# Which head of the attention keeps its norm temporaries apart: from the last one to the second last

## The chip, the cores and the metric

The kernel runs on one core of a Trainium2 chip. The core has five engines with queues of their own: TensorE (PE, matrix products, which it writes to PSUM), VectorE (DVE), ScalarE (ACT), GpSimd (POOL) and SyncE (SP, which here only starts transfers). They run side by side and wait for each other by semaphores. The metric is the device time of one launch in microseconds; a change is judged by the median of its runs beside those of the kernel before.

## The reference

One block of a streaming encoder on 512 rows of width 2048, all in float32: a combined input projection, eight heads of stick-breaking attention, eight heads of forgetting attention, a norm of each head's output, an output projection with residual, and a feed-forward part with squared relu.

```python
def head_rmsnorm(o, g):
    of = o.astype(jnp.float32)
    of = of * lax.rsqrt(jnp.mean(of * of, axis=-1, keepdims=True) + EPS)
    ...

h = rmsnorm(x, g_attn[l])
proj = jnp.einsum('bsd,de->bse', h, w_in[l])
...
o_sb = stick_breaking_attention(qa, ka, va)
o_fox = forgetting_attention(qf, kf, vf, log_f)
mixed = jnp.concatenate([head_rmsnorm(o_sb, g_out_sb[l]),
                         head_rmsnorm(o_fox, g_out_fox[l])], axis=-1)
x = x + jnp.einsum('bse,ed->bsd', mixed, w_out[l])

h2 = rmsnorm(x, g_mlp[l])
u = jax.nn.relu(jnp.einsum('bsd,df->bsf', h2, w_up[l]))
x = x + jnp.einsum('bsf,fd->bsd', u * u, w_down[l])
...
return rmsnorm(x, g_final)
```

## The kernel before

Each float32 operand is split into a high part and the rest: `split` (L56 to L64) lets ScalarE cast the high part (L59) and VectorE subtract it (L60). A product is then three matmuls, high by high, high by low and low by high (`mm3`, L82 to L85). In the profile a product's three matmuls thus carry the lines L83, L84 and L85 whatever they compute, and the tile written tells which: `accv` is the projection to v, `accq` that to q and k, `o` or `oq` the weighted sum of v, `acco` the output projection, `accu` the up and `accd` the down projection.

The heads go in pairs, in the order written in `order`: the eight forgetting heads first, then the stick-breaking heads 0 to 7, so heads 6 and 7 are the last pair. For each head `scores` makes the scores, ScalarE, VectorE and GpSimd turn them into weights `w` in an SBUF tile, and `weigh` (from L213) does the rest:

- TensorE transposes the weights into the PSUM tile `pt` (L218).
- `split` puts them into `ph` (ScalarE, L59) and `pl` (VectorE, L60), each 128 x 1280.
- Twelve matmuls multiply them with v into `o` (L231). For the last head the result is the first bank of a PSUM tile `oq`, whose second bank later takes the sum of squares.
- The head's norm: `os` is the copy of the result (ScalarE, L242), `sq` its square (VectorE, L243), split into `sh` and `sl`; two matmuls with a matrix of ones sum it over the head (L247, L248); `va` is the mean (VectorE, L249); `rsqrt` computes Ln and Exp on ScalarE (L89, L90) and a refining step on VectorE (L91 to L93) in `ra`, `sq` and `va`; the last operation writes `mixed[:, h]` (L251).

`mixed` is the operand of the output projection. That stage takes four blocks of 512 columns, and in each of them eight steps of two heads in the same `order`: weights are loaded and split (`wh`, `wl`), the two heads are split (`uh`, `ul`), and each of four accumulators (one for each 128 rows) takes two times three matmuls. At the end of a block VectorE adds the sums to the residual (L446), ScalarE squares them (L448), and TensorE transposes the new rows (L424) for the next stage.

Tiles come from pools. `wide(name)` gives a tile of 128 x 1280 with a tag of that name from the pool `at`, which holds one buffer for a tag: a new `ph` can be written only when the last reader and writer of the `ph` before is done. In `weigh`, all heads but the last take a second `ph` and `pl` (`n1` and `n2`) for the norm: the first halves hold `sq` and `sh`, the second halves `va` and `sl`. Their `os` and `ra` lie in the tags `ul4` and `uh5` of the pool `up`. The last head has six tiles of 128 x 512 of its own, `os_last` to `sl_last`.

No order is written out by hand: a scheduler puts each engine's instructions in a fixed order when the program is built, by priorities (attention is marked with a high one) and an estimate of its own of when things are ready. That order cannot change on the chip. So the output projection's first matmuls stand between those of the last heads' weighing and norms.

Of the kernel before, what the change touches and what calls it, by code (L numbers as in the profile page):

```python
# [8 lines left out]
F32 = mybir.dt.float32  # L9
F32R = mybir.dt.float32r  # L10
# [4 lines left out]
P = 128  # L15
NT = 512
# [3 lines left out]
NH = 8  # L20
# [16 lines left out]
def block_kernel(ctx, tc, x, g_attn, w_in, b_f, g_out_sb, g_out_fox, w_out, g_mlp, w_up, w_down, g_final, y):  # L37
# [19 lines left out]
    def split(hi, lo, src, scale=None):  # L57
        if scale is None:
            ins = act.copy(hi, src)  # L59
            lows[0] = dve.tensor_tensor(lo, src, hi.bitcast(F32), op=ALU.subtract)  # L60
        else:
            ins = act.mul(hi, src, scale)  # L62
            dve.scalar_tensor_tensor(lo, src, scale, hi.bitcast(F32), op0=ALU.mult, op1=ALU.subtract)
        return ins  # L64
# [5 lines left out]
    def load_w(src, a, b):  # L70

        raw = wp.tile([P, a, b], F32, tag="wraw", name="wraw")
        sp.dma_start(raw, src)
        out = []
        per = min(a, 2 * NT // b)
        for i in range(0, a, per):
            hi, lo = (w.rearrange("p (a b) -> p a b", a=per) for w in hi_lo(per * b))
            split(hi, lo, raw[:, i:i + per, :])
            out += [(hi[:, j, :], lo[:, j, :]) for j in range(per)]
        return out  # L80

    def mm3(out, sh, sl, mh, ml, first, last):  # L82
        pe.matmul(out, sh, mh, start=first, stop=False, skip_group_check=True)  # L83
        pe.matmul(out, sh, ml, start=False, stop=False, skip_group_check=True)  # L84
        pe.matmul(out, sl, mh, start=False, stop=last, skip_group_check=True)  # L85

    def rsqrt(out, v, a, b):

        act.activation(a, v, AF.Ln)  # L89
        act.activation(a, a, AF.Exp, scale=-0.5)  # L90
        dve.scalar_tensor_tensor(b, a, -0.5, v, op0=ALU.mult, op1=ALU.mult)  # L91
        dve.tensor_tensor(b, b, a, op=ALU.mult)
        dve.scalar_tensor_tensor(out, b, 1.5, a, op0=ALU.add, op1=ALU.mult)  # L93
# [29 lines left out]
    g_up, g_sb, g_fx = g_rest[:, :KC], g_rest[:, KC:KC + NH], g_rest[:, KC + NH:]  # L123
# [10 lines left out]
    with (  # L134
# [17 lines left out]
        def accumulate_v(c0, m, steps, prepare=None, more=None):  # L152

            per = NT // m
            banks = [acc.tile([P, NT], F32, tag="acc", name="accv") for _ in range(2)]
            if more is not None:
                banks += [more.tile([P, NT], F32, tag="more", name="accm") for _ in range(2)]
            ps = [banks[t // per][:, t % per * m:(t % per + 1) * m] for t in range(TB)]
            k1 = 0
            for step in steps:  # L160
                k0, k1 = k1, k1 + step
                if prepare is not None:
                    prepare(k0, step)
                w = load_w(w_in[k0 * P:(k0 + step) * P, c0:c0 + m].rearrange("(a p) c -> p a c", p=P), step, m)
                for t in range(TB):
                    ts = slice(t * P, (t + 1) * P)
                    for i in range(step):
                        k = k0 + i
                        mm3(ps[t], hH[:, k, ts], hL[:, k, ts], *w[i], k == 0 and t % per == 0, k == KC - 1)
            return ps  # L170

        def take_v(ps):
            vh = at.tile([P, TB, 2 * P], F32R, tag="vh", name="vh", bufs=2)
            vl = at.tile([P, TB, 2 * P], F32R, tag="vl", name="vl", bufs=2)
            for t in range(TB):
                split(vh[:, t, :], vl[:, t, :], ps[t][:, :2 * P], r1[:, t:t + 1])
            return vh, vl
# [15 lines left out]
        def wide(name, dt=F32):  # L193
            return at.tile([P, 1280], dt, tag=name, name=name)

        def scores(q, k):
            s = atp.tile([P, 1536], F32, tag="s", name="s")
            for i in (3, 2, 0, 1):
                n = (i + 1) * P
                qs = slice(i * P, (i + 1) * P)  # L200
                mm3(s[:, OFF_Q[i]:OFF_Q[i] + n], q[0][:, qs], q[1][:, qs], k[0][:, :n], k[1][:, :n], i != 0, True)
            return s[:, :1280]

        def rows(w):
            return [w[:, OFF_Q[i]:OFF_Q[i] + (i + 1) * P] for i in range(TB)]

        def causal(w, op, fill):

            for d, n in ((w[:, P:1280].rearrange("p (a b) -> p a b", b=384)[:, :, 256:], 3), (w[:, 896:1024], 1)):
                pool.affine_select(out=d, in_=d, compare_op=op, fill=fill, base=0,  # L210
                                   pattern=[[0, n], [-1, P]] if n > 1 else [[-1, P]], channel_multiplier=1)

        def weigh(h, v, hc, w, gv, last=False):  # L213

            pt = atp.tile([P, 1536], F32, tag="s", name="pt")
            for j in range(TB):
                for i in range(j, TB):
                    pe.transpose(pt[:, OFF_T[j] + (i - j) * P:OFF_T[j] + (i - j + 1) * P],  # L218
                                 w[:, OFF_Q[i] + j * P:OFF_Q[i] + (j + 1) * P], ident)
            ph, pl = wide("ph", F32R), wide("pl", F32R)  # L220
            split(ph, pl, pt[:, :1280])
            hs = slice(hc * P, (hc + 1) * P)
            if last:
                oq = atp.tile([P, 1536], F32, tag="s", name="oq")
                o, q = oq[:, :NT], oq[:, NT:2 * NT]
            else:
                o = atp.tile([P, NT], F32, tag="o", name="o")
            for j in range(TB):
                n = NT - j * P
                js = slice(OFF_T[j], OFF_T[j] + n)  # L230
                mm3(o[:, j * P:], v[0][:, j, hs], v[1][:, j, hs], ph[:, js], pl[:, js], j == 0, j == TB - 1)  # L231
            if last:
                os_, sq, va, ra = (at.tile([P, NT], F32, name=f"{c}_last") for c in ("os", "sq", "va", "ra"))
                sh, sl = (at.tile([P, NT], F32R, name=f"{c}_last") for c in ("sh", "sl"))
            else:
                os_ = up.tile([P, NT], F32, tag="ul4", name="os")
                ra = up.tile([P, NT], F32, tag="uh5", name="ra")
                n1, n2 = wide("ph"), wide("pl", F32R)
                sq, va = n1[:, :NT], n1[:, NT:2 * NT]
                sh, sl = n2[:, :NT], n2[:, NT:2 * NT]  # L240
                q = None
            act.copy(os_, o)  # L242
            dve.tensor_tensor(sq, os_, os_, op=ALU.mult)  # L243
            split(sh, sl, sq)
            if q is None:
                q = atp.tile([P, NT], F32, tag="o", name="ssq")
            pe.matmul(q, onesr, sh, start=True, stop=False)  # L247
            pe.matmul(q, onesr, sl, start=False, stop=True)  # L248
            dve.tensor_scalar(va, q, 1.0 / P, EPS, op0=ALU.mult, op1=ALU.add)  # L249
            rsqrt(va, va, ra, sq)  # L250
            dve.scalar_tensor_tensor(mixed[:, h, :], os_, gv, va, op0=ALU.mult, op1=ALU.mult)  # L251

        def attend_sb(h, v, hc, q, k):
            s = scores(q, k)
            w = wide("w")
            act.activation(w, s, AF.Abs)
            act.activation(w, w, AF.Exp, scale=-1.0)
            act.activation(w, w, AF.Ln, bias=1.0)
            dve.scalar_tensor_tensor(w, s, 0.0, w, op0=ALU.max, op1=ALU.add)
            causal(w, ALU.is_gt, 0.0)  # L260
            for r in rows(w):

                dve.tensor_tensor_scan(r[:, ::-1], r[:, ::-1], r[:, ::-1], 0.0, op0=ALU.add, op1=ALU.max)
            dve.tensor_tensor(w, s, w, op=ALU.subtract)
            act.activation(w, w, AF.Exp)
            causal(w, ALU.is_gt, 0.0)
            weigh(h, v, hc, w, g_sb[:, h:h + 1], h == order[-1])

        def attend_fox(h, v, hc, q, k):
            ck = atp.tile([P, NT], F32, tag="o", name="ck")  # L270
# [21 lines left out]
        order = [NH + h for h in (6, 7, 0, 1, 2, 3, 4, 5)] + list(range(NH))  # L292

        def v_columns(h):
            return 2 * WSB + h * P if h < NH else o0 + 2 * WSB + (h - NH) * P
# [61 lines left out]
        with tc.tile_pool(name="attp", bufs=1, space=PSUM) as atp:  # L357
# [9 lines left out]
            v = take_v(ps)  # L367
# [21 lines left out]
            for n in range(0, 2 * NH, 2):  # L389
# [11 lines left out]
                if n:  # L401
                    v = take_v(accumulate_v(v_columns(order[n]), 2 * P, [4] * 4))
# [25 lines left out]
    for n in range(4):  # L428
        ns = slice(n * NT, (n + 1) * NT)
        ps = [acc.tile([P, NT], F32, tag="acc", name="acco") for _ in range(TB)]  # L430
        for k0 in range(0, 2 * NH, 2):
            e0 = order[k0]
            w = load_w(w_out[e0 * P:(e0 + 2) * P, ns].rearrange("(a p) c -> p a c", p=P), 2, NT)
# [141 lines left out]
    for g in range(NG):  # L575
        for db in range(2):
# [6 lines left out]
            for j, p in enumerate(ORDER):  # L583
                if j in steps:
                    job.step()
                w = b_form(p, b)
# [129 lines left out]
```

## Time and profile before

| | |
|---|---|
| median of 3 runs | 2152.41 us (2151.77 to 2153.89) |
| the profiled execution | 2151.46 us |
| its span, first to last instruction | 2149.4 us |
| TensorE busy | 2131.2 us, 99% of the span |
| VectorE busy | 1402.8 us, 65% |
| ScalarE busy | 881.0 us, 41% |
| GpSimd busy | 63.2 us, 3% |
| TensorE's mean granted clock | 0.998 |

In the profile, `out<-in` names the tile written and those read; an instruction's row gives its start in us from the start of the span, its duration, engine, line and operation, and in brackets the idle time of that engine just before it with what ended it. The chain of waits goes back from the last instruction, at each step to what released it. Matmuls are pipelined: their durations overlap, and the distance from start to start tells how fast they follow each other.

### The profile page before, as it was taken

The numbers are of one execution on the slowest core, as the hardware profiler recorded it, in microseconds if no ns is written. First come the engines' busy times: TensorE is split into PE (matmuls) and PEld (weight loads), VectorE is DVE, ScalarE is ACT, GpSimd is POOL, SyncE is SP. The second block draws the span as 40 slices with busy tenths as digits, with TensorE's granted clock in tenths as the row PEclk, the third lists the DMA queues.
The fourth block names the chain that finished last, engine by engine and source line by source line (L and its number), as shares of the span: only waits on it lengthen the run. The fifth ranks groups of instructions, "written<-read, shape, count | busy, mean of one in ns | idle before, by whom it ended". The sixth has DMA issues, their size and how long they took to land.

```text
span 2149.4 us, 25658 instructions
## 1 busy us (share of the span) xinstructions
PE 2131.2 (99%) x10356; PEld 1801.0 (84%) x10356; DVE 1402.8 (65%) x1547; ACT 881.0 (41%) x1146; POOL 63.2 (3%) x75
## 2 busy tenths in 40 slices
PE   9999999999999999999999999999999999999997
PEld 8888988998997888888888888888888888888886
DVE  5455555766566554566776776766776776777788
ACT  6333333444345445443433333333433433433444
POOL 0000000000010000000000000000000000000005
PEclk9999999999999999999999999999999999999999
DMA  6333333322333324233333233233233233233323
GB/s 189 80 84 83 78 83 84 79 79 79 89 112 123 94 93 157 69 118 98 98 114 102 89 117 108 89 114 112 88 108 118 88 99 120 87 101 120 92 70 127
DMA packets 201366, 216.71 MB, mean 101 GB/s; under 512 B 6768, under 2 KB 156832, under 8 KB 201120
## 3 DMA queue, kind: packets, MB, share of 16 engines
q1 hardware_dynamic: 200288, 212.95, 32.9%
q10 hardware_dynamic: 960, 2.13, 0.3%
q8 instruction: 81, 1.33, 0.3%
q14 instruction: 37, 0.30, 0.0%
HBM read 210.86 MB, written 4.19 MB: 100 GB/s over the span
## 4 chain that ended last, share of the span: by engine, by line
PE 96%; DVE 2%; ACT 1%; DMA 1%; issue 0%; POOL 0%; SPq 0%; ACTq 0%; DVEq 0%
PE accu L83 11%; PE accu L84 11%; PE accu L85 11%; PE accd L85 9%; PE accd L83 9%; PE accd L84 9%; PE accq L85 5%; PE accq L83 5%; PE accq L84 5%; PE acco L83 3%; PE acco L84 3%; PE accv L83 3%; PE accv L85 3%; PE acco L85 3%; PE accv L84 3%; PE pt L218 1%
## 5 line engine op out<-in xcount | busy, mean ns | idle before, releaser
L59 ACT CAST wh<-wraw 128x1024 fp32r<-128x1024 f32 (+2 forms) x261 | 270.0, 1035 | 409.9 <-PE accd L85 153.7
L60 DVE TENSOR_TENSOR wl<-wraw,wh 128x1024 fp32r<-128x1024 f32 (+2 forms) x261 | 314.3, 1205 | 166.1 <-ACT wh L59 133.7
L564 DVE TENSOR_TENSOR m<-m,accd 128x1024 f32<-128x1024 f32 x204 | 248.7, 1219 | 263.4 <-PE accd L85 261.7
L83 PE MATMUL accu<-h2h,wh 128*128 128x512 f32 x1024 | 398.6, 389 | 0.0
L84 PE MATMUL accu<-h2l,wh 128*128 128x512 f32 x1024 | 398.4, 389 | 0.0
L85 PE MATMUL accu<-h2h,wl 128*128 128x512 f32 x1024 | 383.7, 389 | 0.0
L59 ACT CAST wh<-wd 128x1024 fp32r<-128x1024 f32 x210 | 219.6, 1052 | 273.6 <-PE accd L85 151.1
L83 PE MATMUL accd<-wh,ufh 128*128 128x512 f32 x840 | 326.8, 389 | 0.0
L84 PE MATMUL accd<-wl,ufh 128*128 128x512 f32 x840 | 326.8, 389 | 0.0
L85 PE MATMUL accd<-wh,ufl 128*128 128x512 f32 x840 | 326.8, 389 | 0.0
L60 DVE TENSOR_TENSOR wl<-wd,wh 128x1024 fp32r<-128x1024 f32 x210 | 255.1, 1221 | 15.1 <-ACT wh L59 13.8
L83 PEld LDWEIGHTS accu<-h2h,wh 128*128 128x128 f32 x1024 | 192.2, 188 | 39.9
L84 PEld LDWEIGHTS accu<-h2l,wh 128*128 128x128 f32 x1024 | 192.2, 188 | 39.8
L85 PEld LDWEIGHTS accu<-h2h,wl 128*128 128x128 f32 x1024 | 192.1, 188 | 39.9
L85 PE MATMUL accq<-hH,wl 128*128 128x512 f32 x512 | 200.8, 392 | 0.0
L83 PE MATMUL accq<-hH,wh 128*128 128x512 f32 x512 | 200.6, 392 | 0.0
L84 PE MATMUL accq<-hL,wh 128*128 128x512 f32 x512 | 200.4, 391 | 0.0
L84 PEld LDWEIGHTS accd<-wl,ufh 128*128 128x128 f32 x840 | 157.7, 188 | 32.8
L85 PEld LDWEIGHTS accd<-wh,ufl 128*128 128x128 f32 x840 | 157.6, 188 | 32.7
L83 PEld LDWEIGHTS accd<-wh,ufh 128*128 128x128 f32 x840 | 157.6, 188 | 32.7
L83 PE MATMUL accv<-wh,hH 128*128 128x256 f32 (+1 forms) x480 | 137.4, 288 | 0.7 <-ACT hH L62 0.7
L84 PE MATMUL accv<-wl,hH 128*128 128x256 f32 (+1 forms) x480 | 135.5, 284 | 0.0
(213 smaller groups left out, 2736.7 us busy)
## 6 DMA issues: line engine op xcount, KB each, us to landing
wraw<-in_w_up_dram SPq DMA_DIRECT2D x128, 512.0 KB, 3.7
wd<-in_w_down_dram SPq DMA_DIRECT2D x120, 512.0 KB, 3.6
wraw<-in_w_in_dram SPq DMA_DIRECT2D x92, 512.0 KB, 3.7
wraw<-in_w_out_dram SPq DMA_DIRECT2D x32, 512.0 KB, 3.6
m<-in_x_dram SPq DMA_DIRECT2D x4, 1024.0 KB, 11.9
wraw<-in_w_down_dram SPq DMA_DIRECT2D x8, 512.0 KB, 4.2
mixed<-in_x_dram SPq DMA_DIRECT2D x2, 1024.0 KB, 10.8
wraw<-in_w_in_dram SPq DMA_DIRECT2D x7, 264.0 KB, 6.8
```

Of the source, the lines that this page charges most:

```text
L59: ins = act.copy(hi, src)
L60: lows[0] = dve.tensor_tensor(lo, src, hi.bitcast(F32), op=ALU.subtract)
L83: pe.matmul(out, sh, mh, start=first, stop=False, skip_group_check=True)
L84: pe.matmul(out, sh, ml, start=False, stop=False, skip_group_check=True)
L85: pe.matmul(out, sl, mh, start=False, stop=last, skip_group_check=True)
L218: pe.transpose(pt[:, OFF_T[j] + (i - j) * P:OFF_T[j] + (i - j + 1) * P], w[:, OFF_Q[i] + j * P:OFF_Q[i] + (j + 1) * P], ident)
L564: dve.tensor_tensor(M[p][:, :, db, :], M[p][:, :, db, :], ps, op=ALU.add)
```

## The change

`weigh` is told how many heads are still to come (`left`) instead of whether its head is the last. For the last head (`left == 0`) only the output copy `os` and the factor `ra` get tiles of their own; its `sq`, `va`, `sh` and `sl` lie in a second `ph` and `pl` as those of the heads before. For the head before it (`left == 1`, head 6) `os` and `ra` stay in the pool `up`, and `n1` and `n2` get tiles of their own of 128 x 1024. All other heads are as before. What is computed does not change, and no instruction is added or removed. From the line of `act.copy(os_, o)` on, lines are one higher in the new file.

```diff
-        def weigh(h, v, hc, w, gv, last=False):
+        def weigh(h, v, hc, w, gv, left=2):
...
-            if last:
+            if left == 0:
                 oq = atp.tile([P, 1536], F32, tag="s", name="oq")
                 o, q = oq[:, :NT], oq[:, NT:2 * NT]
             else:
-                o = atp.tile([P, NT], F32, tag="o", name="o")
+                o, q = atp.tile([P, NT], F32, tag="o", name="o"), None
...
-            if last:
-                os_, sq, va, ra = (at.tile([P, NT], F32, name=f"{c}_last") for c in ("os", "sq", "va", "ra"))
-                sh, sl = (at.tile([P, NT], F32R, name=f"{c}_last") for c in ("sh", "sl"))
+            if left == 0:
+                os_, ra = (at.tile([P, NT], F32, name=f"{c}_last") for c in ("os", "ra"))
             else:
                 os_ = up.tile([P, NT], F32, tag="ul4", name="os")
                 ra = up.tile([P, NT], F32, tag="uh5", name="ra")
+            if left == 1:
+                n1, n2 = at.tile([P, 2 * NT], F32, name="n1"), at.tile([P, 2 * NT], F32R, name="n2")
+            else:
                 n1, n2 = wide("ph"), wide("pl", F32R)
-                sq, va = n1[:, :NT], n1[:, NT:2 * NT]
-                sh, sl = n2[:, :NT], n2[:, NT:2 * NT]
-                q = None
+            sq, va = n1[:, :NT], n1[:, NT:2 * NT]
+            sh, sl = n2[:, :NT], n2[:, NT:2 * NT]
...
-            weigh(h, v, hc, w, g_sb[:, h:h + 1], h == order[-1])
+            weigh(h, v, hc, w, g_sb[:, h:h + 1], NH - 1 - h)
```

## The prediction

> **What bounds the kernel now.** I read the page first, then what TensorE waits for over the whole run, then the chain of waits and the timeline around the one place found.
>
> ```profile
> span 2149.4 us, 25658 instructions
> PE 96%; DVE 2%; ACT 1%; DMA 1%; issue 0%; POOL 0%; SPq 0%; ACTq 0%; DVEq 0%
> ```
>
> The second line is the chain that ended last, by engine: 96% of the span is TensorE (PE) work. A change off TensorE's queue is worth only what TensorE stands still for it. All its recorded waits of the run are these five (total us, times, longest):
>
> ```profile
> PE trg L300 <- DMA g_rows<-in_g_attn_dram: 3.2, 1, 3.2
> PE acco L83 <- ACT uh L59: 2.1, 1, 2.1
> PE tr L149 <- DMA mixed<-in_x_dram: 1.0, 2, 0.8
> PE accv L83 <- ACT hH L62: 0.7, 2, 0.5
> PE acce L84 <- DVE wll L60: 0.4, 1, 0.4
> ```
>
> The first, third and fourth belong to the start, the fifth to the tail. The second is the only stall between them. The chain of waits across it (start, duration):
>
> ```profile
> 681.34 0.69 DVE sq_last L92
> ...
> 682.54 0.69 DVE va_last L93
> ...
> 684.28 0.76 DVE mixed L251
> 685.06 0.63 ACT uh L59
> 685.73 0.50 PE acco L83
> ```
>
> The names ending in `_last` are head 7's norm tiles, the last head in `order`. The output projection is already running (`acco`), and its last head needs `mixed[:, 7]`: L251 writes it, L59 casts it, and only then TensorE goes on. Timeline of TensorE there (start, duration):
>
> ```profile
> 678.06 0.39 PE L83 MATMUL acco<-wh,uh 128*128 128x512 f32 x1
> ...
> 683.27 0.39 PE L85 MATMUL acco<-wh,ul 128*128 128x512 f32 x1
> 685.73 0.50 PE L83 MATMUL acco<-wh,uh 128*128 128x512 f32 x1 [2.07 <-ACT uh L59]
> ...
> 687.68 1.07 PE L85 MATMUL acco<-wh,ul 128*128 128x512 f32 x4
> 688.85 0.66 PE L424 MATMUL tr<-ident,m 128*128 128x128 f32 x4
> ```
>
> Durations overlap, so I count starts. From 678.06 to 683.27 there are 23 steps: 5.21 / 23 = 0.2265 us a matmul. The matmul after 683.27 was due at 683.50 and started at 685.73: **2.23 us lost**. The twelve matmuls from 685.73 should take 2.72 us, but the transposes start 3.12 us later: **0.40 us more**. There the four accumulators end together (the last four matmuls are all L85), so the first transpose has to wait for VectorE's residual addition.
>
> Why head 7 is late:
>
> ```profile
> 660.15 0.75 DVE L251 SCALAR_TENSOR_TENSOR mixed<-os,g_rest,ph 128x512 f32<-128x512 f32 x1
> 660.93 1.23 ACT L59 CAST ph<-pt 128x1280 fp32r<-128x1280 f32 x1 [2.73 <-DVE mixed L251]
> 662.19 1.49 DVE L60 TENSOR_TENSOR pl<-pt,ph 128x1280 fp32r<-128x1280 f32 x1 [1.30 <-ACT ph L59]
> 668.43 0.39 PE L83 MATMUL oq<-ph,vh 128*128 128x512 f32 x1
> ...
> 670.29 0.44 PE L85 MATMUL acco<-wh,ul 128*128 128x512 f32 x1
> ```
>
> Head 6 keeps its norm temporaries (n1, n2) in the tiles `ph` and `pl`. Head 7's weights need the same two tiles, so the cast of head 7 waits until head 6 has written `mixed`. From there to TensorE's first `oq` matmul (668.43) and to the first matmul behind the group (670.29) head 7 is a whole norm behind.
>
> **The change part by part.**
>
> **Head 6's n1 and n2 in tiles of their own.** No instruction is added or removed; the twelve `oq` matmuls, the norm and its four sum matmuls stay. What goes is the wait of `ph<-pt` on L251. In the changed program's order that cast waits for TensorE alone, stands ahead of head 6's `os` copy on ScalarE, and the `oq` group stands 74 matmuls behind the last `accv` matmul instead of 149. So it is a move, and its cover has to be counted. Rows around the new place:
>
> ```profile
> 644.04 0.22 PE L85 MATMUL o<-ph,vl 128*128 128x128 f32 x1
> 644.30 0.59 ACT L242 COPY os<-o 128x512 f32<-128x512 f32 x1 [5.56 <-PE o L85]
> 644.81 1.32 ACT L59 CAST uh<-mixed 128x512 fp32r<-128x512 f32 x2
> 644.92 0.69 DVE L243 TENSOR_TENSOR ph<-os 128x512 f32<-128x512 f32 x1 [4.90 <-ACT os L242]
> 645.53 1.33 DVE L60 TENSOR_TENSOR ul<-mixed,uh 128x512 fp32r<-128x512 f32 x2
> 646.03 1.04 ACT L59 CAST wh<-wraw 128x1024 fp32r<-128x1024 f32 x1
> 647.11 1.23 DVE L60 TENSOR_TENSOR wl<-wraw,wh 128x1024 fp32r<-128x1024 f32 x1 [0.26 <-ACT wh L59]
> 650.75 0.39 PE L83 MATMUL acco<-wh,uh 128*128 128x512 f32 x1
> 651.43 0.39 PE L83 MATMUL acco<-wh,uh 128*128 128x512 f32 x1
> ...
> 654.63 0.63 ACT L89 ACTIVATE ra<-ph 128x512 f32<-128x512 f32 x1 [2.33 <-DVE ph L249]
> 655.29 0.63 ACT L90 ACTIVATE ra<-ra 128x512 f32<-128x512 f32 x1
> 655.94 1.30 ACT L59 CAST uh<-mixed 128x512 fp32r<-128x512 f32 x2
> ```
>
> The last reader of head 6's `ph` is the matmul at 644.04, so ScalarE begins head 7's cast at 644.30: 1.23 us, to 645.53. VectorE's `pl` (1.49 us) then ends near 647.1. The first 73 places hold matmuls of the same sizes in both programs, so place 74 is the start of 651.43: 4.3 us of slack. Queued behind the cast on ScalarE are `os` (0.59), two `uh` (1.32) and `wh` (1.04). The `uh` pair ends near 644.30 + 1.23 + 0.59 + 1.32 = 647.4; TensorE wants it at place 71, 650.75: 3.3 us of slack, the smallest. Behind `pl` on VectorE are head 6's square (0.69), two `ul` (1.33) and `wl` (1.23), done near 650.4; TensorE wants the `ul` only after the `oq` group, near 653.5 (651.43 plus that group's 1.86 us, 668.43 to 670.29). The delay of up to 2.8 us is thus hidden behind matmuls. Without that cover each us beyond 3.3 would stop TensorE. The bounds for this edit are a loss of 0 and one of 2.8 us if nothing covered it; I take 0, since the slack exceeds it.
>
> On ScalarE the copy `os_last<-oq` can now start only when `oq` has ended, near 653.6, and behind it stand head 6's Ln, Exp and the next `uh` pair. TensorE wants that pair at place 135, 48 steps behind the `oq` group: 653.5 + 48 × 0.2265 = 664.4. Copy, Ln, Exp and pair take 0.59 + 0.63 + 0.63 + 1.30 = 3.15 us by the rows above, with VectorE's square and average of head 6 or 7 in between (0.69 each), so they too are covered.
>
> The Trainium skill speaks against such a move: "TensorE: Matmul & The Clock Gate", in the paragraph on engine queue depths of Part 1, has ScalarE and VectorE as strict first-in first-out queues, and only TensorE pulling weight loads forward. By it a late `oq` would block every operand split behind it; if the engines could pass it, the loss would be 0 without any cover. The sum is made with the strict order, and the slack makes both come out alike; it is the slower rival that leans on the rule.
>
> **What the stall becomes.** From the end of `oq` to head 7's write of `mixed` took 684.28 − 670.29 = 14.0 us before. The same from 653.3 gives about 667. TensorE reaches head 7's part of the projection at 683.50, so the 2.23 us go, with some 15 us to spare. Nothing of head 7 is late next.
>
> **The last head's n1, n2 in `ph`, `pl`; its `os` and `ra` apart.** The same operations on other addresses: 0. Head 7's square needs `ph` free, that is its own `oq` matmuls done, which the copy before it already waits for. No later head wants the tiles. The new tiles take as much memory as the old (12 KB a partition), and the four loads of x keep their places in SP's queue; no queue is passed.
>
> **The edge between the first and second column block.** With head 7 in time, the projection's last step runs accumulator by accumulator, so the first addition is done eighteen matmuls before its transposes, and the 0.40 us go. The transposes then stand as four groups of four instead of 4, 4 and 8. The second edge of the old run has that pattern already:
>
> ```profile
> 694.73 0.48 PE L83 MATMUL acco<-wh,uh 128*128 128x512 f32 x1
> ...
> 734.29 0.60 PE L424 MATMUL tr<-ident,m 128*128 128x128 f32 x4
> ...
> 739.42 0.48 PE L83 MATMUL acco<-wh,uh 128*128 128x512 f32 x1
> ```
>
> It takes 5.13 us with 15 matmuls between; the first edge took 694.73 − 688.85 = 5.88 us with 18, which is 5.20 for 15: a gain of 0.07.
>
> **Sum.** 2.23 + 0.40 + 0.07 = 2.70 us. The profiled execution took 2151.46 us (2149.4 span and 2.06 around it), so it becomes 2148.76. It lies 0.95 below the median of the runs shown, 2152.41; on that scale the forecast is **2149.7 us**.
>
> **The rivals.** (a) *Hidden anyway:* the tail or a load takes the 2.7 us back, 2152.4. Against it stands that VectorE, the engine nearest to TensorE's load in the up/down stage, waits for TensorE:
>
> ```profile
> L564 DVE TENSOR_TENSOR m<-m,accd 128x1024 f32<-128x1024 f32 x204 | 248.7, 1219 | 263.4 <-PE accd L85 261.7
> ```
>
> 261.7 us of idle time ended by TensorE means that it starts earlier when TensorE does. For it: the tail is not TensorE's alone. 9%.
>
> (b) *Slower, the wait stays:* `ph` is not freed early after all, while TensorE's order already has `oq` at place 74. `pl` would end at 663.68 as now, TensorE would stand from 651.43 for 12.2 us, with the whole projection queued behind it: 2152.41 + 12.2 − 2.7 = 2161.9. It decides once the weights are more than 4.3 us later than worked out, and ends above the old time from 4.3 + 2.7 = 7.0. This is also the case that the change doesn't do what it says. The changed program's only wait at that cast is TensorE's, so 6%.
>
> (c) *More than the stall:* the gap also slowed what follows it, in the timed executions if not in the profiled one, which was the quickest of all (2151.46 against 2151.77 to 2153.89). The stretches of the profile, with TensorE's granted clock as the column before the last two:
>
> ```profile
> 683.50:685.73 2.23, 0.16 (x2) 0.00 (x1) 2.15 (x4) 1.21 (x2) 0.00 (x0) 1.00 0.20 13
> 685.73:689.30 3.57, 3.47 (x17) 2.62 (x17) 1.86 (x3) 1.14 (x2) 0.00 (x0) 1.00 0.39 139
> ```
>
> The clock stays at 1.00. Were some fifteen matmuls after the gap to run at half rate, that would be 15 × 0.2265 = 3.4 us more to gain: 2152.41 − 2.7 − 3.4 = 2146.3. 9%. "TensorE: Matmul & The Clock Gate" of the Trainium skill (Part 1) halves the clock after an idle window of about 3.4 us; the gap is shorter, and the row agrees.
>
> **How the numbers follow.** Forecast 76%, (a) 9%, (b) 6%, (c) 9%. A measurement of this kernel tells about 0.2%, 4.3 us, from no change. The forecast lies inside that; with runs that spread over 2.1 us, 10 of its 76 read beyond it. Faster: 10 + 9 = 19%. Same: 66 + 9 = 75%. Slower: 6%. The range takes in (a) and a spread of about 2 us below the forecast: 2147.6 to 2152.7, with (b) and most of (c) left out.
>
> **What would show it.** Right: no wait of `acco` on `uh` in the list of TensorE's waits; head 7's cast starting near 644.3 without VectorE as releaser; `oq` from about 651.4 to 653.3; head 7's L251 (a line later in the new file) near 667; the first transposes near 686.2 instead of 688.85, and every later stage earlier by 2.6 to 2.7. Wrong: a new wait of TensorE between 650 and 690, above all at `oq` or the first `uh` behind it, or an unchanged start of the tail.

## The result, and the profile after

| | median (us) | lowest to highest | runs |
|---|---|---|---|
| before | 2153.2 | 2151.77 to 2154.4 | 20 |
| changed | 2149.22 | 2148.45 to 2150.38 | 20 |

The ratio is 0.9982, 95% interval 0.9975 to 0.9989. The medians are 4.0 us apart and the means 3.8 us; the interval reaches from 2.4 to 5.4 us. The profiled execution took 2148.76 us against 2151.46, that is 2.70 less. So the profiled executions differ by the predicted sum, though not by its terms alone (the spans differ by 2.4 us, 2149.4 against 2147.0; more on this below), and the timed runs by about 1.1 us more. Most of what follows is about that remainder.

The page of the changed kernel, with the chain that ended last by engine, and its list of what TensorE waits for:

```profile
span 2147.0 us, 25661 instructions
PE 96%; DVE 2%; ACT 1%; issue 0%; POOL 0%; DMA 0%; SPq 0%; ACTq 0%; DVEq 0%
```

```profile
PE trg L301 <- DMA g_rows<-in_g_attn_dram: 3.3, 1, 3.3
PE tr L149 <- DMA mixed<-in_x_dram: 1.3, 2, 1.1
PE accv L83 <- ACT hH L62: 0.7, 2, 0.5
PE acce L84 <- DVE wll L60: 0.5, 1, 0.5
```

The other four waits are still there; the row of `acco` on `uh` is gone and none has taken its place. ScalarE and VectorE in the timeline of the changed kernel, from head 7's cast to head 7's write of `mixed`:

```profile
644.51 1.23 ACT L59 CAST ph<-pt 128x1280 fp32r<-128x1280 f32 x1 [5.56 <-PE o L85]
...
645.77 1.49 DVE L60 TENSOR_TENSOR pl<-pt,ph 128x1280 fp32r<-128x1280 f32 x1 [5.55 <-ACT ph L59]
...
646.11 1.15 ACT L59 CAST uh<-mixed 128x512 fp32r<-128x512 f32 x2
...
653.70 0.59 ACT L243 COPY os_last<-oq 128x512 f32<-128x512 f32 x1 [1.19 <-PE oq L85]
...
661.21 1.22 DVE L60 TENSOR_TENSOR wl<-wraw,wh 128x1024 fp32r<-128x1024 f32 x1
662.34 0.68 DVE L250 TENSOR_SCALAR ph<-oq 128x512 f32<-128x512 f32 x1
...
663.97 0.62 ACT L59 CAST uh<-mixed 128x512 fp32r<-128x512 f32 x1 [0.28 <-PE acco L84]
664.49 0.63 ACT L90 ACTIVATE ra_last<-ra_last 128x512 f32<-128x512 f32 x1
...
668.90 0.75 DVE L252 SCALAR_TENSOR_TENSOR mixed<-os_last,g_rest,ph 128x512 f32<-128x512 f32 x1
```

The cast `ph<-pt` starts at 644.51 instead of 660.93, released by TensorE's last `o` matmul and no longer by `mixed`. TensorE in the same kernel's timeline:

```profile
651.65 0.39 PE L83 MATMUL oq<-ph,vh 128*128 128x512 f32 x1
...
653.50 0.44 PE L248 MATMUL ssq<-n,onesr 128*128 128x512 f32 x1
...
683.49 0.39 PE L85 MATMUL acco<-wh,ul 128*128 128x512 f32 x1
683.72 0.39 PE L83 MATMUL acco<-wh,uh 128*128 128x512 f32 x1
...
686.21 0.40 PE L85 MATMUL acco<-wh,ul 128*128 128x512 f32 x1
686.44 0.60 PE L425 MATMUL tr<-ident,m 128*128 128x128 f32 x4
...
691.58 0.48 PE L83 MATMUL acco<-wh,uh 128*128 128x512 f32 x1
```

At 683.49 TensorE passes without a stop over the place where it had stood for 2.23 us, and the transposes begin at 686.44 instead of 688.85.

### The profile page after: what moved, and what is told of

Same layout as the page of the kernel before. It is cut to its first block, busy times and chain, and to the rows that moved or that the text cites. A ratio compares the mean times of both kernels' runs of the same rounds, so it can differ in the third digit from the quotient of the medians.

```text
span 2147.0 us, 25661 instructions
## 1 busy us (share of the span) xinstructions
PE 2130.7 (99%) x10356; PEld 1801.2 (84%) x10356; DVE 1403.0 (65%) x1547; ACT 880.0 (41%) x1146; POOL 63.2 (3%) x75
## 4 chain that ended last, share of the span: by engine, by line
PE 96%; DVE 2%; ACT 1%; issue 0%; POOL 0%; DMA 0%; SPq 0%; ACTq 0%; DVEq 0%
PE accu L83 11%; PE accu L85 11%; PE accu L84 11%; PE accd L83 9%; PE accd L84 9%; PE accd L85 9%; PE accq L85 5%; PE accq L83 5%; PE accq L84 5%; PE acco L85 3%; PE acco L83 3%; PE acco L84 3%; PE accv L83 3%; PE accv L85 3%; PE accv L84 3%; PE pt L218 1%
```

## The experiments

Each kernel was timed beside the kernel before on the same chip. "The gap" below is TensorE's stop ahead of head 7's part of the projection, from the start of the last matmul before it to the start of the next, less one step of 0.23 us.

**The second half of the change alone.** The last head's norm lies in `ph` and `pl`; head 6 shares its tiles as before.

```diff
             if last:
-                os_, sq, va, ra = (at.tile([P, NT], F32, name=f"{c}_last") for c in ("os", "sq", "va", "ra"))
-                sh, sl = (at.tile([P, NT], F32R, name=f"{c}_last") for c in ("sh", "sl"))
+                os_, ra = (at.tile([P, NT], F32, name=f"{c}_last") for c in ("os", "ra"))
+                n1, n2 = wide("ph"), wide("pl", F32R)
+                sq, va = n1[:, :NT], n1[:, NT:2 * NT]
+                sh, sl = n2[:, :NT], n2[:, NT:2 * NT]
```

> The second half of the change alone: the last head keeps only its output and one factor apart and takes ph and pl for the rest, head 6 goes on sharing ph and pl. TensorE's order is that of the kernel before. Theory (the whole gain is head 6's two tiles, this half only pays for their memory): no gain, within 0.5 us of the kernel before, the stall of TensorE on head 7's operand stays at 2.0 to 2.5 us. Rival (the last head's new places help too): over 1 us faster.

2153.37 us (2151.64 to 2154.75, 11 runs), ratio 0.9999 (0.9991 to 1.0008). Its wait of `acco` on `uh` is 2.1 us, as before, and from the last `accv` matmul to the first transposes it takes 689.38 − 637.16 = 52.22 us, also as before. This half is worth nothing by itself.

**The first half alone.** Head 6's temporaries in tiles of their own, as in the change; the last head's `sq` and `va` in a tile of their own, its `sh` and `sl` in the tile `w`, since six separate tiles do not fit beside head 6's two.

```diff
+            if left == 1:
+                n1, n2 = at.tile([P, 2 * NT], F32, name="n1"), at.tile([P, 2 * NT], F32R, name="n2")
+            elif left == 0:
+                n1, n2 = at.tile([P, 2 * NT], F32, name="n1_last"), wide("w", F32R)
+            else:
                 n1, n2 = wide("ph"), wide("pl", F32R)
```

> The first half of the change alone: head 6 has n1 and n2 of its own, and the last head's norm temporaries stay out of ph and pl (its sq and va in a tile of their own, sh and sl in the weights' tile w, which is free by then, since memory does not hold all six). TensorE's order is that of the changed kernel. Theory (this half is the gain): the time of the changed kernel, 2149.2 us within 0.5, no stall of TensorE on uh. Rival (both halves are needed): more than 1 us slower than the changed kernel.

2149.38 us (2148.45 to 2150.36, 11 runs), ratio 0.9983 (0.9974 to 0.9992): the whole gain, as far as the runs can tell. Its first transposes, by the timeline, stand where the changed kernel has them:

```profile
686.45 0.60 PE L427 MATMUL tr<-ident,m 128*128 128x128 f32 x4
```

**The changed tiles with the old order.** The changed kernel, with head 7's `oq` group held back in TensorE's order behind the projection's fifth step; the dependency is one of order alone, without a semaphore.

```diff
     def mm3(out, sh, sl, mh, ml, first, last):
-        pe.matmul(out, sh, mh, start=first, stop=False, skip_group_check=True)
+        ins = pe.matmul(out, sh, mh, start=first, stop=False, skip_group_check=True)
...
+        return ins
...
+                if left == 0 and j == 0:
+                    held.append(ins)
...
+            if n == 0 and k0 == 8:
+                tc.add_manual_dep(held[0].ins, ins.ins.name, mybir.DependencyInfo(mybir.DependencyClass.NoSync, mybir.DependencyReason.DATA), reason="late")
```

> The changed kernel with head 7's weighing held back in TensorE's order to place 143, near its old place 149: the tiles are free early, the order is nearly the old one. Theory (the gain comes through the order, which the scheduler could move because the tiles are free): the stall comes back, 0.5 to 2.5 us, and most of the gain is gone: 2150.5 to 2153 where the kernel before takes 2153. Rival (freeing the tiles is enough, the order does not matter): the time of the changed kernel, 2149.2.

2152.92 us (2151.73 to 2154.74, 11 runs), ratio 1.0 (0.9991 to 1.0009). Its timeline:

```profile
667.04 0.39 PE L85 MATMUL oq<-ph,vh 128*128 128x512 f32 x1
...
684.24 0.75 DVE L257 SCALAR_TENSOR_TENSOR mixed<-os_last,g_rest,ph 128x512 f32<-128x512 f32 x1
...
685.70 0.50 PE L85 MATMUL acco<-wh,uh 128*128 128x512 f32 x1 [2.07 <-ACT uh L59]
```

The tiles are those of the change, `oq` starts 15.4 us later than in it, and the stall is back. So the free tiles give nothing unless the order uses them. The hold also let the scheduler place other engines' work anew; it is TensorE's order together with what follows from it that is shown to matter.

**The kernel before once more,** and **the gap closed in another way:** the old tiles and TensorE's old order, with the last head's norm leaving out the three VectorE operations that refine the reciprocal root (L91 to L93).

```diff
-            rsqrt(va, va, ra, sq)
+            if last:
+                act.activation(ra, va, AF.Ln)
+                act.activation(ra, ra, AF.Exp, scale=-0.5)
+                va = ra
+            else:
+                rsqrt(va, va, ra, sq)
```

> The kernel before once more, for a second profile. Plain theory (the stall costs only its own length): a profile like the first, the stall at 2.1 to 2.3 us, the matmuls behind it 0.227 us apart and the granted clock at 1.00, and times that scatter for reasons outside this stretch. Rival (the gap also slows what follows it in some executions): a profiled execution over 2153 us shows the clock below 1.00 and matmuls further apart than 0.227 us just behind the gap; one under 2152 us does not.

> The kernel before, where the last head leaves out the refining step of its reciprocal root (three VectorE operations), so that its output is ready some 4 us earlier in the same order of TensorE. No stall should be left; the four accumulators still end together. Plain theory: faster by the stall and its restart, 2.2 to 2.5 us. Rival (the gap also slows what follows in some executions): faster by 3.3 to 4 us, and its times scatter as little as those of the changed kernel (1.2 us without outliers) instead of 2.6 us.

The kernel before again took 2153.33 us (2151.19 to 2154.95, 11 runs), ratio 1.0 (0.9991 to 1.0009). Its profiled execution took 2151.97 us and has the clock at 1.00 behind the gap; both theories expect that of an execution under 2152 us, so it decides nothing between them. The short norm took 2149.75 us (2149.0 to 2150.59, 11 runs), ratio 0.9984 (0.9975 to 0.9993), 1.5 to 5.4 us less. Its stretch across the old gap (columns: stretch and its length, then busy time and count of TensorE, its weight loads, VectorE, ScalarE and GpSimd, the granted clock, DMA share and GB/s) shows TensorE busy throughout:

```profile
680.00:688.00 8.00, 8.00 (x37) 6.46 (x35) 5.47 (x8) 5.22 (x8) 0.00 (x0) 1.00 0.40 116
```

Closing the gap with old tiles and old order thus gives what the change gives. The gain comes from the gap; and here too the timed runs gained more, 3.4 us by the ratio, than the 2.4 us that the trace shows (from the last `accv` matmul to the first transposes 688.31 − 638.46 = 49.85 us, against 52.22 before). The interval takes in both forecasts, 2.2 to 2.5 us and 3.3 to 4 us, and so doesn't choose between them; the times do spread over 1.6 us only, where those of the kernel before beside it spread over 3.8.

**The gap made shorter and longer.** If a gap has a price beyond its length, it shows when the length is varied. All four are the kernel before with the last head's norm changed: shorter by leaving out the multiplication of L92, longer by one, three or six multiplications of head 7's `mixed` by 1.0. TensorE's order is that of the kernel before across the gap and for 7 us behind it; after that a few matmuls stand in other places with one and with six multiplications more.

```diff
+            if last:
+                act.activation(ra, va, AF.Ln)
+                act.activation(ra, ra, AF.Exp, scale=-0.5)
+                dve.scalar_tensor_tensor(sq, ra, -0.5, va, op0=ALU.mult, op1=ALU.mult)
+                dve.scalar_tensor_tensor(va, sq, 1.5, ra, op0=ALU.add, op1=ALU.mult)
```

```diff
             dve.scalar_tensor_tensor(mixed[:, h, :], os_, gv, va, op0=ALU.mult, op1=ALU.mult)
+            if last:
+                for _ in range(1):
+                    dve.tensor_scalar(mixed[:, h, :], mixed[:, h, :], 1.0, None, op0=ALU.mult)
```

> The kernel before, where the last head leaves out one VectorE multiplication of its reciprocal root (L92): the stall should shrink from 2.2 us to about 1.0 us, in the same order of TensorE. Plain theory (the stall costs its own length): about 1.2 us faster than the kernel before, with its scatter. Rival (a gap of 2.2 us also slows what follows it in some executions, a shorter one in fewer): 1.7 to 2.7 us faster, with fewer executions in the upper half of the scatter.

> The kernel before with one more VectorE operation on the last head's output (multiplied by 1.0), in the same order of TensorE: the stall grows by what that operation takes, 0.4 to 0.7 us. Plain theory: the time grows by the same. Rival: by more, 0.7 to 1.5 us, since a longer gap slows what follows more often.

> As before with three such operations: stall 3.4 to 4.3 us. Plain theory: the time of the kernel before plus 1.2 to 2.1 us, clock 1.00 behind the gap. Rival: a drop of the granted clock in the profile behind the gap in most executions, and 0.4 to 1.7 us more than the stall's growth.

> As before with six such operations: stall 4.6 to 6.4 us. Plain theory: the time grows by the stall's growth, 2.4 to 4.2 us. Rival: the granted clock is below 1.00 behind the gap in the profile, matmuls there start up to 0.45 us apart, and the time grows by 1 to 2 us more than the stall.

| | gap in the profile (us) | median, range, runs (us) | ratio, interval | clock behind the gap |
|---|---|---|---|---|
| shorter | 1.2 | 2151.19, 2150.1 to 2152.04, 11 | 0.9993, 0.9984 to 1.0002 | 1.00 |
| before | 2.2 | 2152.12, 2151.32 to 2154.61, 31 | | |
| one more | 3.2 | 2155.52, 2152.26 to 2156.66, 11 | 1.0011, 1.0002 to 1.0019 | half |
| three more | 4.1 | 2154.98, 2154.1 to 2156.45, 11 | 1.0012, 1.0003 to 1.0021 | half |
| six more | 5.5 | 2157.82, 2156.12 to 2158.24, 9 | 1.0024, 1.0014 to 1.0033 | half |

The stretches behind the gap, first with the gap shortened, then with one and with six multiplications more:

```profile
685.00:688.00 3.00, 3.00 (x12) 2.17 (x12) 1.58 (x4) 0.62 (x1) 0.00 (x0) 1.00 0.57 175
```

```profile
687.00:688.00 1.00, 1.00 (x5) 0.84 (x4) 0.34 (x1) 0.00 (x0) 0.00 (x0) 0.88 0.31 119
688.00:691.00 3.00, 3.00 (x8) 2.16 (x7) 0.97 (x2) 0.87 (x2) 0.00 (x0) 0.50 0.00 0
```

```profile
685.00:687.00 2.00, 0.00 (x0) 0.00 (x0) 2.00 (x4) 0.32 (x1) 0.00 (x0) 0.97 0.07 7
687.00:690.00 3.00, 0.00 (x0) 0.00 (x0) 2.33 (x6) 0.46 (x1) 0.00 (x0) 0.50 0.47 170
690.00:693.00 3.00, 2.79 (x7) 2.22 (x8) 0.69 (x1) 0.15 (x1) 0.00 (x0) 0.50 0.00 0
```

These rows count 12 matmuls in three microseconds at full clock, and 7 or 8 in three at half clock. In the one profile of each, the gap of 3.2 us was followed by half clock and the gap of 1.2 us was not. The medians jump where the executions of a kernel differ in this; by the means the four kernels take 1.5 us less and 2.2, 2.6 and 4.9 us more than the kernel before beside them, where their gaps are 1.1 us shorter and 0.9, 1.9 and 3.2 us longer.

For the shortened gap that is between the plain forecast of 1.2 us and the rival's 1.7 to 2.7, within an interval that takes in both. The single multiplication made the gap 0.9 us longer, not 0.4 to 0.7 as expected. Not every timed execution with it paid: the fastest, 2152.26 us, is below the sum of 2151.46 us and the 0.93 us of added gap, which leaves no room for a further price. That three multiplications cost no more than one can't be told by these runs, whose intervals overlap almost wholly. Half-clock time that falls into the idle gap is free, as the last rows show for the kernel with six; in the one profile of the kernel with three, all of it came behind the gap.

**The kernel before three times more, profiled.** The gap of 2.2 us lies between, and the one execution shown ahead of the change had full clock. Either the executions differ there, or they scatter only by how late they start.

> The kernel before, for a further profile of its 2.2 us gap. Theory (the gap halves TensorE's clock for about 3.4 us in about half of the executions): if this execution takes over 2153.2 us, the profile shows the granted clock at 0.5 for some us behind 685 and matmuls 0.43 us apart; if it takes under 2152.2 us, 1.00 and 0.227 us. Rival (the scatter comes from the start alone): the clock is 1.00 whatever the time.

> The same as the run before: clock 0.5 behind the gap if over 2153.2 us by the theory, 1.00 in any case by the rival.

> The same again: clock 0.5 behind the gap if over 2153.2 us by the theory, 1.00 in any case by the rival.

Stretches of the same kernel in these three executions, which took 2152.00, 2154.49 and 2153.34 us:

```profile
684.00:686.00 2.00, 0.20 (x1) 0.00 (x0) 2.00 (x3) 1.02 (x2) 0.00 (x0) 1.00 0.06 4
686.00:689.00 3.00, 2.73 (x12) 2.18 (x12) 1.20 (x3) 0.80 (x2) 0.00 (x0) 1.00 0.50 172
```

```profile
685.00:687.00 2.00, 0.12 (x1) 0.00 (x0) 2.00 (x3) 1.03 (x2) 0.00 (x0) 1.00 0.19 12
687.00:690.00 3.00, 2.82 (x7) 2.26 (x8) 0.77 (x2) 0.13 (x1) 0.00 (x0) 0.57 0.49 167
```

```profile
684.00:686.00 2.00, 0.01 (x1) 0.00 (x0) 1.98 (x3) 1.03 (x2) 0.00 (x0) 1.00 0.08 6
686.00:689.00 3.00, 2.92 (x7) 2.34 (x8) 0.69 (x1) 0.03 (x1) 0.00 (x0) 0.50 0.50 171
```

The program and the gap are the same in all three, and in two of them the clock halves behind it. What that costs is read from the second of the three, in TensorE's timeline:

```profile
687.18 0.59 PE L83 MATMUL acco<-wh,uh 128*128 128x512 f32 x1 [2.07 <-ACT uh L59]
...
691.88 0.55 PE L424 MATMUL tr<-ident,m 128*128 128x128 f32 x3
```

From the first matmul behind the gap to the first transpose it takes 4.70 us, against 3.12 at full clock: 1.58 lost. In the third it is 1.53.

The rest is the start. Take 2151.46 us, add how much later than 636.63 the last `accv` matmul starts (that much the front of the kernel is late), and add the half-clock loss:

| execution | start later | half clock | sum | measured |
|---|---|---|---|---|
| third | 0.54 | 0 | 2152.00 | 2152.00 |
| fourth | 1.46 | 1.58 | 2154.50 | 2154.49 |
| fifth | 0.35 | 1.53 | 2153.34 | 2153.34 |

With the change of the gap as a further term, the sum meets the one-, three- and six-multiplication kernels' profiled executions within 0.11 us as well. The start alone would leave 1.5 us open in two of the three.

**What decides whether the gap is caught.** The trace's record of the clock gives the moment of each change. In the fifth execution the clock falls at 686.01 and comes back 3.41 us later, at 689.42; its next fall, behind the last matmuls of the program, is at 2143.50, that is 1457.49 us after the first. In the fourth execution and in the kernels with one and three multiplications more, the fall behind the gap (687.45, 687.76, 689.09) also lies 1457.5 us ahead of the last one, which is 427 times 3.4133 us; with six, the half clock lasts twice 3.41 us (686.88 to 693.71). So the clock changes on a grid with steps of 3.413 us, and the grid lies differently against the gap in each execution. Counted back from the last fall, the grid can be placed where the clock did not drop as well. Rows of one step each, first of the kernel before as profiled ahead of the change, then of its fifth execution, then of the kernel with three multiplications:

```profile
681.62:685.04 3.42, 2.04 (x10) 1.34 (x8) 3.42 (x6) 1.32 (x2) 0.00 (x0) 1.00 0.00 0
685.04:688.45 3.41, 2.72 (x12) 2.17 (x12) 1.62 (x3) 1.19 (x2) 0.00 (x0) 1.00 0.53 154
```

```profile
682.59:686.01 3.42, 1.42 (x7) 0.84 (x5) 3.39 (x5) 1.30 (x3) 0.00 (x0) 1.00 0.05 4
686.01:689.42 3.41, 3.34 (x8) 2.66 (x9) 0.69 (x1) 0.02 (x1) 0.00 (x0) 0.50 0.44 150
```

```profile
682.26:685.68 3.42, 1.69 (x8) 1.08 (x6) 3.42 (x6) 0.98 (x2) 0.00 (x0) 1.00 0.00 0
685.68:689.09 3.41, 1.21 (x5) 1.01 (x6) 2.12 (x5) 0.62 (x1) 0.00 (x0) 1.00 0.45 154
689.09:692.50 3.41, 3.41 (x11) 2.48 (x10) 1.33 (x3) 0.67 (x2) 0.00 (x0) 0.50 0.00 0
```

TensorE's idle time in a step is its length less the first busy time. In the first execution the gap is cut by a step's end into 1.38 and 0.69 us, and the clock stays; in the fifth nearly all of it, 2.00 us, lies in one step, and the next step is at half clock; with three multiplications 1.73 us in one step did nothing and 2.20 us in the next did. The other profiles of this stretch agree: each of the six steps with 1.98 us or more of idle time was followed by half clock, and no step with 1.73 us or less. Where the limit lies between these two was not measured. If the grid may lie anywhere, a gap with 2.07 us of idle time is caught in (3.41 − 2.07 + 2 × (2.07 − limit)) / 3.41 of the executions: 45 to 60% with a limit from 1.98 to 1.73, an estimate from these profiles.

## Why the prediction was right, point by point

**Head 6's tiles free head 7's weights: right.** The cast came at 644.51 (predicted 644.3), `oq` ran from 651.65 to 653.50 (651.4 to 653.3); about 0.2 us of each difference is the later start of this execution, 636.85 against 636.63. The first half alone carries the gain.

**Its cover: right.** `pl` ended at 647.26 (647.1) and the `uh` pair at 647.26 (647.4), both more than 3 us ahead of TensorE's need.

**Head 7's `mixed` near 667: 2 us too early.** It was written at 668.90. From the end of `oq` it took 15.4 us (668.90 − 653.50) and not the 14.0 us of before; the rest is the later start and the rounding of 667.3. The prediction took that time over whole, and did not count whom head 7's operations would stand behind in the new place. VectorE's mean (L250) stands behind the split of the next weights (661.21), and comes 1.1 us later after `oq` than before. Head 7's Exp stands behind a `uh` cast that waits for TensorE at 663.97, and starts at 664.49, 0.8 us after the Ln before it had ended. Both fit the strict order of the engines' queues, which the prediction had weighed for the operand splits and not for these instructions. Later steps gave 0.5 us back. With 14 us to spare it cost nothing.

**The last head's tiles: right,** 0 predicted; the second half alone has the ratio 0.9999 and the same 52.22 us in the profile.

**The three terms: right.** From the last `accv` matmul to the first transposes it takes 49.59 us (686.44 − 636.85), against 52.22 before (688.85 − 636.63): 2.63 less, where the stall and the restart were put at 2.23 + 0.40. The first edge takes 691.58 − 686.44 = 5.14 us with 15 matmuls, 0.06 less than the 5.20 reckoned from before; put at 0.07. Two sizes hide in this. The prediction laid the whole 0.40 to the four accumulators that end together. In the run with the short norm they still do, without a gap, and from the first of the twelve matmuls to the transposes it takes 688.31 − 685.33 = 2.98 us, 0.26 more than 2.72; the other 0.14 goes with the gap, and lies in the slower restart behind it (the first two starts at 685.73 and 686.07 are 0.34 us apart). And that the profiled executions differ by 2.70 to the hundredth is luck: the three terms gave 2.69, the changed execution started 0.22 later, so the later stages came 2.47 earlier (the second edge's transposes at 731.82 instead of 734.29) and not 2.6 to 2.7, and another 0.25 us came from outside the span, where the prediction had taken 2.06 us for both kernels and the changed one has 1.8.

**Rivals (a) and (b): fallen.** The tail took nothing back (2.47 us at the second edge, 2.4 in the span), and no wait appeared between 650 and 690.

**The scale of the timed runs: the step that failed.** The forecast took the profiled 2.70 us off the median of the runs, and held (c), a price behind the gap, for unlikely on one row, a clock of 1.00. That row was one execution. The mechanism of (c) was real in part of the executions, with a price of 1.5 to 1.6 us and not the 3.4 us of fifteen half-rate matmuls: the half clock lasted 3.41 us, which is time for 8 half-rate matmuls and not for fifteen, and the twelve matmuls behind the gap lost 1.58 us. How often it struck in the timed runs can only be bounded. Of the 79 runs of the kernel before that stood beside the experiments, 19 have a mean clock of 0.997, and each of these took 2153.11 us or more; of the changed kernel's 20 runs, all have 0.998 or 0.999. Of these 79 and the 20 of the result, 46 took over 2153.2 us, some of them by a late start alone. A quarter to a half of 1.55 us is 0.4 to 0.7; the estimate of 45 to 60% above leans to the upper end. With the 2.69 us of the three terms and the 0.25 us outside the span that makes 3.3 to 3.6 of the measured 3.8 us; the interval spans 2.4 to 5.4, so what is left cannot be told from scatter. That the forecast of 2149.7 was only 0.5 us high is luck in part: the median that it started from was 0.8 us below that of the larger number of runs, and its gain 1.3 us below that of the medians, and the two errors work against each other.

The Trainium skill, "TensorE: Matmul & The Clock Gate", Part 1, halves the clock after an idle window of about 3.4 us, and says that the window runs freely. The prediction used the length alone, by which 2.2 us was safe. The runs do not agree with the length as a threshold: 2.2 us was enough in two of seven profiled executions with that gap. They agree with a window of 3.413 us that runs freely, by the grid above; but a window need not be idle as a whole, since 1.98 us of idle time in one of them was enough.

## What to carry to other kernels

In a program whose order is fixed when it is built, freeing a buffer pays only if the order moves with it: compare where TensorE's instructions stand, and count matmul starts up to the place where the data are needed. A short stop of TensorE can cost more than its length, and only in some executions; profile the same kernel several times before reading the clock behind a gap as fixed. To find out whether a gap is worth closing, make it longer and shorter by an operation or two: that prices it without building the cure.

## What the runs showed of the hardware

- The half-clock stretch need not begin where TensorE starts again. With the gap of 2.2 us it set in within 0.3 us of the first matmul; with 4.1 us the first microsecond behind the gap ran at 1.00 (the first row below, stretches of that kernel); with 5.5 us the clock fell near 687, some 2 us after TensorE had stopped, and 3.3 us of the half-clock time passed idle. Even so the matmuls behind that gap lost 1.60 us, as much as behind the gap of 2.2 us, since the half clock lasted 6.83 us there, two steps of the grid.

```profile
688.00:689.00 1.00, 1.00 (x5) 0.81 (x6) 0.56 (x1) 0.00 (x0) 0.00 (x0) 1.00 0.00 0
689.00:692.00 3.00, 3.00 (x9) 2.19 (x8) 0.83 (x2) 0.62 (x1) 0.00 (x0) 0.52 0.00 0
```

- The execution is longer than its span by an amount that is steady within a kernel and differs between kernels: 1.7 to 1.8 us where the gap is gone (the changed kernel, its first half alone, the short norm), 1.9 with the gap shortened, 2.0 to 2.1 in the kernel before and with one and six multiplications more, but 1.8 with three. So it doesn't follow the gap, and its cause was not tried. It makes up 0.25 us of the measured gain.
